# The check for experts over capacity placed in front of the last expert

## The chip, the cores and the metric

One core of one Trainium2 chip runs the whole program. The metric is device time in microseconds (us), the median over executions, and the reference's result has to be reproduced. An execution holds TensorE (PE, with its weight loads as PEld), VectorE (DVE), ScalarE (ACT), GpSimd (POOL) and SyncE (SP); SP issues nearly all the DMA transfers. A name with q behind it in a row (SPq, PEldq, DVEq, ACTq) is the instruction queue of that engine.

## The reference, cut to what matters

Two encoder layers over 256 tokens of width 1024. The first layer ends in a dense SwiGLU, the second in a layer of eight experts, of which each token uses two. The change lies in that expert layer:

```python
def moe_swiglu(h, router_w, w1, w3, w2):
    logits = (xf @ router_w).astype(jnp.float32)
    top_val, top_idx = lax.top_k(logits, TOP_K)          # 2 of 8 experts for each token
    gates = jax.nn.softmax(top_val, axis=-1)
    ...
    def expert_block(args):
        xblk, e = args
        return (jax.nn.silu(xblk @ w1[e]) * (xblk @ w3[e])) @ w2[e]
    ...
    out = jnp.zeros((n, d), h.dtype).at[buf_tok].add(yb * buf_g[:, None].astype(yb.dtype))
```

After it the layer's output is normalised, multiplied by a gate vector and added to the residual stream, which is the program's output.

## The kernel before, in words

The expert layer is `moe_layer`. Each of the eight experts has 42 pieces of weights of 1 MB. `weights` (L973) gives each piece a buffer and issues its DMA from SP (L978). The buffers form a ring of 18 in program order (L970): three and four that earlier stages used (`raw`, `hl`) and eleven of its own (`mw`).

An expert is planned for at most 96 tokens (`CAP`), in three groups of 32 slots. `gather` (L1040) makes its input: two DVE instructions build a one-hot matrix `oh`, 32 matmuls in four steps put the chosen tokens into `gx`, and eight ACT instructions write them, scaled and shifted, to `xe`. `oh` and `xe` have two buffers each.

The hidden width 3584 is worked through in four units `s` (L31: 256, 256, 256 and 128 columns of each of four parts of 896). `up` (L1104) multiplies `xe` with eight (in the last unit four) pieces of w1 and w3 into the accumulators `u`; `gated` (L1133) makes silu(a)*b on ACT and DVE and transposes it; `down` (L1145) multiplies that with four (at last two) pieces of w2 into `y`. `run` (L1230) is a pipeline: the `down` of a unit stands behind the `up` of the next unit, over the border between two experts as well. When the last `down` of an expert is out, `finish_tasks` splits `y` in two parts (`outputs`, L1167) and `back` (L1174) brings the slots back to token rows with 24 matmuls into `cb` and adds them, times the gate, to the sum `yac` on DVE (L1188). These tasks are given out between the pieces of the next expert's first `up`; those of the last expert come at the end.

The third group of slots is computed under a run-time branch on PE alone (`rest`, L1086, the branch at L1092): an expert with up to 64 tokens jumps over it.

`more` (L1258) hands further tasks to `run`: in the unit `s == 1` of each expert the gather of the next one (`prepare`), and in the first unit of the last expert the broadcast of the gate vector to `gtB`.

Experts with more tokens than 96 are handled by a general path. `count` makes a list of them; `over(0)` (L1276) loads its first entry into a register of every engine (L1277) and enters the branch `tc.If(ov > 0)` (L1278). Its body runs a whole expert again for the surplus, with its own gather and 42 pieces of weights, and holds `over(1)` up to `over(4)` inside, so the code of five experts stands in it. The body takes buffers of the same weight ring and of `oh`, `xe`, `u`, `y` and `yac`, in program order, whether it is entered or not. In the kernel before this call (L1303) stands behind all eight experts and in front of `residual` (L346): four ACT squares with row sums (`junk`, L299), 1/sqrt by Ln and Exp (L290, L291), four DVE products with `gtB` (L350), four DVE sums (L353) and the output DMAs (L355).

A planner orders the instructions of each engine by its own estimate of when they can start, so an instruction may stand earlier than in the program text when it needs nothing that comes in between; what is inside a branch is not mixed with what is outside.

Of the kernel before, what the change touches and what calls it, by code (L numbers as in the profile page):

```python
# [26 lines left out]
NE = 8  # L27
# [93 lines left out]
def kernel(ctx, tc, x, cc, cst, cst2, msk, ada, pcol, lora, poolw, rpb, win, winl, wout,  # L121
# [151 lines left out]
    def use_lnexp():  # L273

        pl = act.preload_act_table_set("natural_log_exp_and_others")
        if pin["last"] is not None:
            tc.add_manual_dep(pl.ins, pin["last"].ins.name, NOSYNC, reason="table set after its last user")
        pin["pl"] = pl
# [685 lines left out]
    def moe_layer(l):  # L964
        with ExitStack() as st:
# [74 lines left out]
            def gather(pos):  # L1040

                oh = ep.tile([128, 2, CAP], F32, name="oh", tag="oh", bufs=2)
                for tb in range(2):
                    dve.tensor_scalar(oh[:, tb, :], C("iota")[:, 0:CAP], pos[:, tb:tb + 1], rs[:, tb:tb + 1],
                                      op0=OP.is_equal, op1=OP.mult)
                xe = ep.tile([128, KB, CAP], F32, name="xe", tag="xe", bufs=2)

                def step(k2):
                    p = pa("gx").rearrange("p (j t) -> p j t", j=2)[:, :, 0:CAP]
                    for j in range(2):  # L1050
                        ks = slice((2 * k2 + j) * 128, (2 * k2 + j + 1) * 128)
                        for tb in range(2):
                            mm(p[:, j, :], xr[:, tb, ks], oh[:, tb, :], tb == 0, tb == 1)
                    for j in range(2):
                        k = 2 * k2 + j
                        act.activation(xe[:, k, :], p[:, j, :], AF.Identity,  # L1056
                                       scale=gcol[l][:, 2, k:k + 1], bias=mods[l][:, SH_F, k:k + 1])

                return xe, [lambda k2=k2: step(k2) for k2 in range(KB // 2)]
# [14 lines left out]
            def slot_map(x):  # L1074

                x.oT = one.tile([128, NG, T], F32R, name="oT", tag="oT")
                dve.tensor_tensor(x.oT, x.row[:, None, :].to_broadcast([128, NG, T]),
                                  C("slot")[:, :, None].to_broadcast([128, NG, T]), op=OP.is_equal)
# [25 lines left out]
            def up(x, s, tasks):  # L1104

                w = SUP[s]
                kk = 256 // w
                n0 = sum(KB * SUP[i] // 256 for i in range(s))
                us = [pb("u") for _ in range(NG)]

                def part(n, pc, gs):
                    for i in range(kk):
                        k = n * kk + i
                        for g in gs:
                            for j in range(4):
                                mm(us[g][32 * j:32 * j + 32, 0:2 * w],
                                   x.xe[:, k, 32 * g:32 * g + 32],
                                   pc((i * 4 + j) * 2 * w, 2 * w), k == 0, k == KB - 1)

                for m in range(0, KB // kk, BATCH):  # L1120
                    pcs_ = []
                    for n in range(m, m + BATCH):
                        pcs_.append((n, weights(x.src(n0 + n))))
                        part(*pcs_[-1], range(GB))
                        if tasks:
                            tasks.pop(0)()
                    x.rest(lambda: [part(n, pc, range(GB, NG)) for n, pc in pcs_],
                           (lambda: [clear(us[g]) for g in range(GB, NG)]) if m == 0 else None)
                while tasks:
                    tasks.pop(0)()  # L1130
                return us

            def gated(s, us):  # L1133
                w = SUP[s]
                sgs = []
                for u in us:
                    sg = ep.tile([128, 256], F32, name="sg", tag="sg", bufs=NG)[:, 0:w]
                    other_set(act.activation(sg, u[:, 0:w], AF.Silu))  # L1138
                    dve.tensor_mul(sg, sg, u[:, w:2 * w])  # L1139
                    sT = ep.tile([128, 256], F32, name="sT", tag="sT", bufs=2 * NG)[:, 0:w]  # L1140
                    dve.transpose(sT, sg)
                    sgs.append(sT)
                return sgs
# [46 lines left out]
            def finish_tasks(x, first):  # L1190
                outputs(x)
                return [lambda tb=tb: back(x, tb, first) for tb in range(2)]
# [27 lines left out]
            def fixed(e):  # L1220
                return lambda n: moe[e * NCH + n]
# [4 lines left out]
            def prepare(e):  # L1226
                xes[e], steps = gather(posm[:, :, e])
                return steps

            def run(units, extra_tasks=None):  # L1230

                prev = None
                tasks = []
                for x, s, first in units:
                    if s == 2:
                        slot_map(x)
                    if extra_tasks is not None:
                        tasks += extra_tasks(x, s)
                    us = up(x, s, tasks)
                    tasks = []  # L1240
                    aT = gated(s, us)
                    if prev is not None:
                        px, ps_, paT, pfirst = prev
                        down(px, ps_, paT)
                        if ps_ == len(SUP) - 1:
                            tasks = finish_tasks(px, pfirst)
                    prev = (x, s, aT, first)
                px, ps_, paT, pfirst = prev
                down(px, ps_, paT)
                for f in finish_tasks(px, pfirst):  # L1250
                    f()
# [5 lines left out]

            def more(x, s):  # L1258
                e = x.gi
                if s == 1 and e + 1 < NE:  # L1260
                    return prepare(e + 1)
                if e == 0 and s == 0:
                    return [lambda: rows_of(prow, posm, NE)]
                if e == NE - 1 and s == 0:
                    return [lambda: bcast_col(gtB, gcol[l][:, 3, :], pa)]
                return []

            def units():
                for e in range(NE):
                    x = Expert(fixed(e), prow[:, e, :], gate[:, :, e], e, xes[e], nt[0:1, e:e + 1])  # L1270
                    for s in range(len(SUP)):
                        yield x, s, e == 0

            run(units(), more)

            def over(i):  # L1276
                ov = nc.values_load(of[0:1, i:i + 1], min_val=0, max_val=1)  # L1277
                with tc.If(ov > 0):  # L1278
                    base = nc.sync.value_load(ox[0:1, i:i + 1], min_val=0, max_val=(NE - 1) * NCH)

                    def src(n):
                        return moe[bass.ds(base + n, 1)].rearrange("o p f -> p (o f)")

                    es = one.tile([128, NE], F32, name="es", tag="es")
                    dve.tensor_scalar(es, it8, oif[:, i:i + 1], None, op0=OP.is_equal)
                    pe2 = one.tile([128, 2, 2], F32, name="pe2", tag="pe2")
                    tmp = one.tile([128, NE], F32, name="etmp", tag="etmp")
                    for tb in range(2):
                        for q, a in ((0, posm), (1, gate)):
                            dve.scalar_tensor_tensor(tmp, a[:, tb, :], 1.0, es, op0=OP.mult, op1=OP.mult,  # L1290
                                                     accum_out=pe2[:, q, tb:tb + 1])
                    dve.tensor_scalar(pe2[:, 0, :], pe2[:, 0, :], osec[:, i:i + 1], None, op0=OP.subtract)
                    xe, steps = gather(pe2[:, 0, :])
                    for f in steps:
                        f()
                    orow = one.tile([128, 1, T], BF, name="orow", tag="orow")
                    rows_of(orow, pe2[:, 0, :, None], 1)
                    x = Expert(src, orow[:, 0, :], pe2[:, 1, :], NE + i, xe)
                    run(((x, s, False) for s in range(len(SUP))))
                    if i < NOV - 1:  # L1300
                        over(i + 1)

            over(0)  # L1303
            use_lnexp()
            residual([[yac[:, tb, h] for h in HALF] for tb in range(2)], out)

# [24 lines left out]
    if stop == 3:  # L1331
        nc.sync.dma_start(out, xr)
        return
    moe_layer(1)


# [118 lines left out]
```

## Time and profile before

| what | us |
|---|---|
| three runs | 1490.93, 1497.38, 1497.62 (median 1497.38) |
| profiled execution | 1491.34 |
| its span, first to last instruction | 1489.6 |
| PE, DVE, ACT busy | 1385.4, 610.0, 399.2 |
| expert layer's weights | 336 pieces of 1 MB |

The span is that of the profiled execution; its own time is 1.74 us longer. Busy PE time is modelled and includes matmuls that run half empty, so a high share of it does not say that PE is the bound of a stretch. Weights of the experts move from about 630 us on to 1470 us.

### The profile page before, as it was taken

What the parts mean: (1) busy time and instruction counts of PE and PEld (TensorE: products, weight loads), DVE (VectorE), ACT (ScalarE), POOL (GpSimd) and SP (SyncE); (2) the same over time, 40 slices, a digit from 0 to 9 for tenths busy, and PEclk for the clock granted to TensorE, in tenths of its full rate; (3) what the DMA queues carried; (4) which work ended last, traced back from release to release, by engine and by line L of the source; (5) the groups of instructions that cost most, each with busy time, mean ns of one, the idle gap of its engine ahead of it and who ended that gap; (6) DMA issues with size and microseconds to landing.
All of it is one profiled execution on the core that took longest, in us unless ns stands there. A gap on an engine that the chain in (4) does not pass through costs nothing. (4 is left out here: it accounts for less than half of the span.)

```text
span 1489.6 us, 30982 instructions
## 1 busy us (share of the span) xinstructions
PE 1385.4 (93%) x13669; PEld 818.1 (55%) x13694; DVE 610.0 (41%) x1198; ACT 399.2 (27%) x774; POOL 1.9 (0%) x19
## 2 busy tenths in 40 slices
PE   3999989999998999989998899999999999999874
PEld 2997769999997997743332233333333433333221
DVE  7698879878856786440020120021020200200203
ACT  4744465444437644231020010010010010010101
POOL 0000000000000000000000000000000000000000
PEclk9999999999999999999999999999999999999998
DMA  9554559977734420499999999999999999999993
GB/s 370 219 195 144 183 224 392 387 294 306 298 141 149 149 94 17 170 407 419 419 420 420 419 420 420 420 419 420 420 419 419 420 420 420 420 419 419 420 420 139
DMA packets 70286, 487.43 MB, mean 327 GB/s; under 512 B 8177, under 2 KB 8561, under 8 KB 12658
## 3 DMA queue, kind: packets, MB, share of 16 engines
q1 hardware_dynamic: 68546, 482.45, 80.1%
q10 hardware_dynamic: 1584, 2.68, 0.6%
q8 instruction: 125, 2.05, 0.5%
q14 instruction: 31, 0.25, 0.0%
HBM read 484.05 MB, written 1.05 MB: 326 GB/s over the span
## 5 line engine op out<-in xcount | busy, mean ns | idle before, releaser
L167 PE MATMUL u<-mw,xe 128*32 128x512 f32 (+1 forms) x4864 | 491.1, 541 | 24.0 <-DMA mw<-in_moe_dram 16.3
L167 PEld LDWEIGHTS u<-mw,xe 128*32 128x32 f32 x4864 | 157.8, 110 | 299.3 <-issue 237.8
L1139 DVE TENSOR_TENSOR sg<-sg,u 128x256 f32<-128x256 f32 (+1 forms) x96 | 34.0, 382 | 587.3 <-ACT sg L1138 587.3
L167 PE MATMUL y<-mw,sT 128*32 128x512 f32 x2128 | 243.0, 594 | 15.7 <-DMA mw<-in_moe_dram 10.3
L218 DVE TENSOR_TENSOR whl<-raw,whl 128x1024 fp32r<-128x1024 f32 x142 | 170.2, 1221 | 50.8 <-ACT whl L217 50.5
L1138 ACT ACTIVATE sg<-u 128x256 f32<-128x256 f32 (+1 forms) x96 | 30.7, 356 | 570.5 <-PE u L167 559.6
L217 ACT ACTIVATE whl<-raw 128x1024 fp32r<-128x1024 f32 x142 | 147.0, 1057 | 114.6 <-issue 51.5
L167 PEld LDWEIGHTS y<-mw,sT 128*32 128x32 f32 x2128 | 71.1, 110 | 174.4 <-issue 129.6
L170 PE MATMUL g<-hhi,whl 128*128 128x256 f32 x448 | 127.3, 284 | 0.0
L171 PE MATMUL g<-hlo,whl 128*128 128x256 f32 x448 | 127.2, 284 | 0.1
L172 PE MATMUL g<-hhi,whl 128*128 128x256 f32 x448 | 127.0, 284 | 0.0
L254 DVE CUSTOM_DVE_ANT_0 raw<-raw,row,pcs 128x1024 f32<-128x1024 f32 x96 | 120.2, 1278 | 4.6 <-ACT row L1311 3.9
L170 PE MATMUL z<-hhi,whl 128*128 128x256 f32 x304 | 88.1, 290 | 4.6 <-ACT whl L217 3.9
L172 PE MATMUL z<-hhi,whl 128*128 128x256 f32 x304 | 86.4, 284 | 2.4 <-DVE whl L218 2.4
L171 PE MATMUL z<-hlo,whl 128*128 128x256 f32 x304 | 86.6, 285 | 0.5 <-DVE hlo L336 0.3
L170 PEld LDWEIGHTS g<-hhi,whl 128*128 128x128 f32 x448 | 86.5, 193 | 0.6
L171 PEld LDWEIGHTS g<-hlo,whl 128*128 128x128 f32 x448 | 86.3, 193 | 0.8 <-DVE hlo L336 0.4
L172 PEld LDWEIGHTS g<-hhi,whl 128*128 128x128 f32 x448 | 86.3, 193 | 0.0
L170 PEld LDWEIGHTS z<-hhi,whl 128*128 128x128 f32 x304 | 58.0, 191 | 6.5 <-ACT whl L217 4.2
L172 PEld LDWEIGHTS z<-hhi,whl 128*128 128x128 f32 x304 | 58.0, 191 | 3.1 <-DVE whl L218 3.0
L171 PEld LDWEIGHTS z<-hlo,whl 128*128 128x128 f32 x304 | 58.1, 191 | 2.1 <-DVE hlo L336 1.1
L1056 ACT ACTIVATE xe<-gx,mods,gcol 128x96 f32<-128x96 f32 x64 | 24.1, 428 | 121.4 <-PE gx L167 121.2
(290 smaller groups left out, 1484.0 us busy)
## 6 DMA issues: line engine op xcount, KB each, us to landing
mw<-in_moe_dram SPq DMA_DIRECT2D x336, 1024.0 KB, 19.9
raw<-in_ada_dram SPq DMA_DIRECT2D x44, 1024.0 KB, 7.0
raw<-in_ffn_dram SPq DMA_DIRECT2D x42, 1024.0 KB, 7.2
raw<-in_win_dram SPq DMA_DIRECT2D x20, 1024.0 KB, 4.8
raw<-in_wout_dram SPq DMA_DIRECT2D x6, 1024.0 KB, 4.8
raw<-in_ada_dram SPq DMA_DIRECT2D x8, 512.0 KB, 7.4
bi<-in_rpb_dram ACTq DMA_DIRECT2D x8, 256.0 KB, 2.8
raw<-in_wout_dram SPq DMA_DIRECT2D x4, 512.0 KB, 3.6
```

Source lines behind the costliest of these rows:

```text
L167: pe.matmul(o, a, b, start=start, stop=stop)
L170: pe.matmul(o, ah, bh, start=start, stop=False)
L171: pe.matmul(o, ah, bl, start=False, stop=False)
L172: pe.matmul(o, al, bh, start=False, stop=stop)
L217: ops[0].append(act.activation(hi, raw[:, c], AF.Copy))
L218: ops[1].append(dve.tensor_sub(lo, raw[:, c], hi.bitcast(F32)))
L254: r = dve.tensor_tensor_reduce(w, w, cB, scale=1.0, scalar=P(l, "ab", v * KB + k), op0=OP.mult, op1=OP.add, accum_out=mods[l][:, v, k:k + 1])
L1056: act.activation(xe[:, k, :], p[:, j, :], AF.Identity, scale=gcol[l][:, 2, k:k + 1], bias=mods[l][:, SH_F, k:k + 1])
L1138: other_set(act.activation(sg, u[:, 0:w], AF.Silu))
L1139: dve.tensor_mul(sg, sg, u[:, w:2 * w])
```

## The change

`over(0)` is called after seven experts instead of after eight. The pipeline `run` is called twice: once for the experts 0 to 6 and once for the expert 7. Between the two stand the check and the gather of expert 7, whose four steps are called one after another; before, they were handed out among the pieces of expert 6. Nothing is computed differently.

```diff
             def more(x, s):
                 e = x.gi
-                if s == 1 and e + 1 < NE:
+                if s == 1 and e + 1 < NE - 1:
                     return prepare(e + 1)
...
-            def units():
-                for e in range(NE):
+            def units(es):
+                for e in es:
                     x = Expert(fixed(e), prow[:, e, :], gate[:, :, e], e, xes[e], nt[0:1, e:e + 1])
                     for s in range(len(SUP)):
                         yield x, s, e == 0
-
-            run(units(), more)
...
+            run(units(range(NE - 1)), more)
             over(0)
+            for f in prepare(NE - 1):
+                f()
+            run(units(range(NE - 1, NE)), more)
             use_lnexp()
             residual([[yac[:, tb, h] for h in HALF] for tb in range(2)], out)
```

## Rows read from the trace of the kernel before

**Rows 1.** The page: span, the DMA line of the 40 slices, the weight transfers

```profile
span 1489.6 us, 30982 instructions
...
DMA  9554559977734420499999999999999999999993
...
mw<-in_moe_dram SPq DMA_DIRECT2D x336, 1024.0 KB, 19.9
```

**Rows 2.** Busy time by stretch; last: PE clock, DMA share, GB/s

```profile
800.00:900.00 100.00, 90.39 (x850) 30.15 (x847) 13.61 (x32) 7.81 (x21) 0.00 (x0) 1.00 1.01 420
1300.00:1400.00 100.00, 93.86 (x852) 34.74 (x854) 15.81 (x35) 9.86 (x25) 0.00 (x0) 1.00 1.01 419
```

**Rows 3.** Waits of SP's queue: total us, times, longest

```profile
SPq L978 <- DMA mw<-in_moe_dram: 582.9, 285, 3.7
...
SPq L978 <- PEq L1092: 9.6, 4, 6.9
```

**Rows 4.** Timeline, end of the last expert: start, us, what, idle before

```profile
1458.11 1.92 PE L167 MATMUL y<-mw,sT 128*32 128x512 f32 x16 [0.55 <-DMA mw<-in_moe_dram]
...
1470.59 1.93 PE L167 MATMUL y<-mw,sT 128*32 128x512 f32 x16 [0.46 <-SPq L1278]
...
1473.10 2.99 PE L167 MATMUL cb<-yhl,oT 64*128 64x512 f32 x22 [0.16 <-DVE yhl L1172]
...
1474.80 2.73 DVE L1188 SCALAR_TENSOR_TENSOR yac<-cb,gate,yac 128x512 f32<-128x512 f32 x4 [0.90 <-PE cb L167]
1479.83 0.63 ACT L299 ACTIVATE junk<-yac 128x512 bf16<-128x512 f32 x1 [4.82 <-DVEq L1278]
```

**Rows 5.** The check's line L1278 by engine: duration ns, first and last start

```profile
L1278 SPq EVENT_SEMAPHORE  x9: 17/17/17, 1455.8 to 1470.8; - x9
...
L1278 PEldq EVENT_SEMAPHORE  x2: 51/51/51, 1477.9 to 1478.0; - x2
L1278 DVEq EVENT_SEMAPHORE  x2: 21/21/21, 1479.8 to 1479.9; - x2
...
L1278 SPq COMPARE_BRANCH  x1: 45/45/45, 1450.5 to 1450.5; - x1
...
L1278 PEldq COMPARE_BRANCH  x1: 3370/3370/3370, 1474.4 to 1474.4; - x1
L1278 DVEq COMPARE_BRANCH  x1: 72/72/72, 1476.8 to 1476.8; - x1
```

**Rows 6.** The weight DMAs of L978, issue to landing over all 336

```profile
DMA to landing us min/median/max: 4.8/19.9/21.5
```

**Rows 7.** Timeline, tail after the check on DVE and SP

```profile
1480.59 0.69 DVE L350 TENSOR_TENSOR yac<-yac,row 128x512 f32<-128x512 f32 x1 [3.06 <-ACT junk L299]
...
1482.68 0.68 DVE L350 TENSOR_TENSOR yac<-yac,row 128x512 f32<-128x512 f32 x1
...
1483.29 2.73 DVE L353 SCALAR_TENSOR_TENSOR xr<-yac,rs,xr 128x512 f32<-128x512 f32 x4
```

**Rows 8.** Timeline, the first expert's gather: DVE, then PE

```profile
643.41 0.56 DVE L1044 TENSOR_SCALAR oh<-cs,posm,rs 128x96 f32<-128x96 f32 x2
643.78 5.44 PE L167 MATMUL gx<-oh,xr 128*128 128x96 f32 x32 [0.71 <-DVE oh L1044]
```

**Rows 9.** Timeline of expert 6 on PE, and its border to expert 7

```profile
1302.89 1.13 PE L167 MATMUL gx<-oh,xr 128*128 128x96 f32 x8
...
1323.98 1.16 PE L167 MATMUL bc<-cs,gcol 128*128 128x128 f32 x8
...
1331.91 7.08 PE L167 MATMUL u<-mw,xe 128*32 128x512 f32 x64 [0.25 <-issue]
...
1369.58 1.92 PE L167 MATMUL u<-mw,xe 128*32 128x512 f32 x16 [0.55 <-DMA mw<-in_moe_dram]
```

**Rows 10.** Busy time by stretch at the end; third last: PE clock

```profile
1478.00:1480.00 2.00, 0.00 (x0) 0.00 (x0) 0.00 (x0) 0.17 (x1) 0.00 (x0) 1.00 0.03 8
1480.00:1482.00 2.00, 0.00 (x0) 0.00 (x0) 1.42 (x4) 2.00 (x8) 0.00 (x0) 0.66 0.01 4
1482.00:1484.00 2.00, 0.00 (x0) 0.00 (x0) 1.95 (x5) 1.17 (x5) 0.00 (x0) 0.50 0.00 0
```

## The prediction

> **What bounds the kernel now.** I read the page first. Its DMA line stands at 9 in the slices from about 17 to 39: from some 630 us on the core does nothing faster than it can load weights, 336 pieces of 1 MB [rows 1]. The table by stretches says the same in numbers: the DMA share is 1.01 at 419 to 420 GB/s in any 100 us of the expert layer [rows 2], so a piece of 1.049 MB costs 2.50 us. The timeline of the last expert shows it from the other side. PE needs 1.92 us for a piece and then waits for the next one; from the pieces that start at 1458.11 to the one at 1470.59 there are five steps, 12.48 / 5 = 2.50 us each [rows 4]. SP issues a piece when one of eight in flight has landed (285 waits for the transfers themselves), and only rarely waits for a buffer [rows 3]; eight times 2.50 us are the 19.9 us that a piece takes to land [rows 1]. So the layer's time is that of an unbroken stream of transfers, and whatever PE, ACT and DVE do in it is free until it breaks the stream. Last I read the rows of the check's own line and the tail, where the stream has ended and everything is exposed [rows 4, 5, 7].
>
> **What the check does where it stands now.** No instruction of the body was executed: no expert is over capacity, each engine jumps. The jump isn't free. PE meets it at 1474.4 while its last matmuls still run, is held 3.37 us, and signals at 1477.9 that it is past. DVE meets it at 1476.8 and signals at 1479.8. SP is the first, at 1450.5, and then executes nine event instructions, the last at 1470.8, just when the last piece has landed: it waits there for its transfers in flight, one after another [rows 5]. And later work waits for these signals as if the body had run. ACT's first square needs the sum `yac`, whose first quarter is finished by 1475.5, but starts at 1479.83, released by DVE's signal [rows 4].
>
> **Part 1, the check out of the tail: a gain of 3.0 us.** Without it the squares start as the quarters of `yac` arrive. ACT could so begin 1479.83 - 1475.5 = 4.3 us earlier, but DVE can't follow: its four sums L1188 last until 1474.80 + 2.73 = 1477.53 [rows 4], and behind them stand the products and sums of the residual, which run from 1480.59 without a real gap to 1483.29 + 2.73 = 1486.02 [rows 7]. That 5.4 us block now starts when DVE is free and at least one square has read its quarter, so at about 1477.55 instead of 1480.59: 3.0 us. What is late next is DVE itself. Bounds: 0, if the residual's order changes for the worse, and 4.3. The load of the ACT table that stands there now lies beside DVE's sums and stays so.
>
> **Part 2, the check between experts 6 and 7: a loss of 9.6 us.** Every weight DMA of expert 7, 42 of them, is now behind the check in SP's queue, and behind it in the buffers too: the ring's last users in program order are the matmuls of the body. The rows give two possible ends of SP's wait. Its own events, 0.2 us after the last piece (1470.8 against 1470.59) [rows 4, 5], are the lower one. The upper one is the signal of an engine that uses the buffers, that is PE: 1477.9 - 1470.59 = 7.3 us after the last piece of the expert begins on PE. I take PE's. It is what happened to ACT with DVE's signal [rows 4], and SP's weight DMAs are already seen waiting for PE's signal at the small branch L1092, four times, up to 6.9 us [rows 3]. If SP had to wait for the slowest engine, DVE, it would be 9.2 us.
>
> Then the queue is empty. A piece that meets an empty queue lands 4.8 us after its issue, the smallest of the 336 values [rows 6]. So expert 7's first piece is there 7.3 + 4.8 = 12.1 us after the last piece of expert 6, where the unbroken stream needed 2.50. The difference is 9.6 us. All 41 others follow at 2.50 us, so this is shifted to the end in full. Nothing of the 10 us is won back by the buffers that are free: they can't be filled before PE's signal. Bounds by SP's wait: 0.2 + 4.8 - 2.5 = 2.5 us and 9.2 + 4.8 - 2.5 = 11.5 us.
>
> The chain between last piece and signal is the one seen at the end, with expert 6 in place of expert 7: matmuls, `outputs`, 24 matmuls of `back` ending at 1476.09, the jump. Before, these lay between the pieces of expert 7. Expert 6 could enter it late: PE works there without waiting for weights and meets the stream again at 1369.58 in expert 7 [rows 9]. But PE loses work in expert 6, the gather of 32 matmuls (four times 1.13 us [rows 9]), so I expect it level with the stream; the bound is some 1.5 us more.
>
> [...] PE was held 3.37 us by the jump [rows 5], and its matmuls in the queue ended 1.8 us before the signal. [...]
>
> **Part 3, the gather of expert 7: nothing.** In expert 6 its matmuls filled time under the stream, so taking them out there gives nothing. In the new place it waits for DVE's signal at +9.2 us, then 0.56 us for `oh` and 5.4 us for 32 matmuls [rows 5, 8]: PE is ready at about +15.2 us, 3.1 us after the first piece. It catches up: unhindered it takes 7.08 / 4 = 1.8 us for a piece [rows 9] against 2.50, so 0.7 us a piece, five pieces of 42. [...] The broadcast to `gtB` was moved by the planner into expert 6 already [rows 9] and is free in either place.
>
> **Sum.** -3.0 + 9.6 + 0 = +6.6 us. On the profiled execution's own time, 1491.34 (span 1489.6 and 1.74 around it), that is 1497.9, or 0.44% more. The three runs lie in two groups, one like the profiled execution, two some 6.2 us above it; nothing in the profile says which the changed kernel will meet, so I put the sum on their mean, 1495.3: 1501.9.
>
> **Rivals.**
> - SP waits only for its own transfers. For it: the nine events are the only thing SP is seen waiting for at L1278. Against: ACT's wait for DVE's signal. Then 2.5 - 3.0 = -0.5, 1494.8.
> - The planner takes expert 7's weights past the check, so that the stream isn't broken: it does move work past small branches, as the `bc` row inside expert 6 shows [rows 9]. Against: buffers of the ring that the body uses. Then -3.0, 1492.3. It is the only faster case, and less than 0.5%.
> - The tail doesn't give back its 3.0 us, since DVE puts the residual in another order or waits for the last square. Then +9.6, 1504.9.
> - Slower still, by PE: the gather behind the jump becomes the bound. It is exposed after DVE's signal, and it decides if PE can't win back its delay before the last piece, that is if a piece of expert 7 costs PE 2.4 us or more, as with the third group of slots computed. Then 3.1 (or, at the lower clock, 8.5) comes on top: +9.7 to +15.1, 1505.0 to 1510.4. Against: at the end of expert 7 PE needs 1.92 us a piece [rows 4]. [...]
>
> **How the numbers follow.** Chances: forecast 0.60, SP free of PE 0.10, stream unbroken 0.05, tail without gain 0.13, PE's delay 0.12. A measurement of this kernel tells about 0.5% (7.5 us) from no change. The forecast lies 0.9 us below that line, with its own range from +5 (a cheaper jump) to +8.5 (SP held to DVE's signal), so about 0.4 of its chance is slower and the rest the same. Slower: 0.60 x 0.4 + 0.13 + 0.12 = 0.49, of which I take off a little for the two groups of runs, which can hide it: 0.45. Faster by over 0.5% is reached by no case, 0.05 for what I don't see. Same 0.50. The range leaves out the unbroken stream below and the slowest form of PE's delay by a little: 1494 to 1511.
>
> **What would show it.** In the changed profile: SP's events of the check's line near 1365 us and then no weight issue until PE's second signal, some 7 us later; a hole in the DMA line of about 10 us; in the tail, squares that start on `yac` itself and DVE going from L1188 to L350 without its 3.06 us pause. The prediction is wrong if weights are issued before PE's signal, if PE waits less than 0.3 us for pieces at the end of expert 7, or if the hole is under 6 or over 13 us.

## The result and the profile after

| | before | changed |
|---|---|---|
| median of 12 runs each, us | 1496.38 (1490.93 to 1497.62) | 1504.01 (1499.34 to 1506.82) |
| ratio | | 1.0056, 95% interval 1.0045 to 1.0068 |
| profiled execution, us | 1491.34 | 1505.6 |
| its span, us | 1489.6 | 1503.8 |

The change makes the kernel 7.6 us slower by the medians, 8.4 by the ratio (6.7 to 10.2 by the interval); +6.6 us and 1501.9 had been forecast. The two profiled executions lie 14.2 us apart, which is more than the change does. So the stages are compared from one instruction that both kernels have before they differ, the first of expert 5's `cb` matmuls. It stands at 1291.79 before and at 1296.70 after: the first 4.9 us of the 14.2 have nothing to do with the change.

```profile
1291.79 1.60 PE L167 MATMUL cb<-yhl,oT 64*128 64x512 f32 x6
```

```profile
1296.70 1.60 PE L167 MATMUL cb<-yhl,oT 64*128 64x512 f32 x6
```

From there to PE's start on the last piece of weights it takes 178.80 us before (1470.59 [rows 4]) and 191.24 after (1487.94, below): +12.4. From there to the end of the span 19.0 and 15.9: -3.1. Together +9.3 in this pair of executions.

The page of the changed kernel, the lines that answer to [rows 1]:

```profile
span 1503.8 us, 31010 instructions
...
DMA  9554459987734420499999999999999999995995
...
mw<-in_moe_dram SPq DMA_DIRECT2D x336, 1024.0 KB, 19.9
```

The row of nines has a 5 in it. The busy time by stretch shows what it is (columns as in [rows 2], the last ones PE clock, DMA share and GB/s):

```profile
1300.00:1365.00 65.00, 60.99 (x586) 20.28 (x582) 9.58 (x23) 2.80 (x9) 0.00 (x0) 1.00 0.95 391
1365.00:1378.00 13.00, 7.73 (x64) 3.56 (x56) 4.80 (x7) 1.79 (x3) 0.00 (x0) 1.00 0.13 50
```

For 13 us the core loads 50 GB/s in place of 420. The check's line, now L1276, answers to [rows 5]:

```profile
L1276 SPq EVENT_SEMAPHORE  x9: 17/17/17, 1355.0 to 1370.2; - x9
...
L1276 PEldq EVENT_SEMAPHORE  x2: 51/51/51, 1377.1 to 1377.2; - x2
L1276 DVEq EVENT_SEMAPHORE  x2: 21/21/21, 1379.1 to 1379.3; - x2
...
L1276 SPq COMPARE_BRANCH  x1: 50/50/50, 1349.9 to 1349.9; - x1
...
L1276 PEldq COMPARE_BRANCH  x1: 3333/3333/3333, 1373.7 to 1373.7; - x1
```

And the timeline of the border between the experts 6 and 7 (start, us, engine, line, idle before with its releaser):

```profile
1363.53 1.93 PE L167 MATMUL y<-mw,sT 128*32 128x512 f32 x16 [0.56 <-DMA mw<-in_moe_dram]
...
1369.81 1.92 PE L167 MATMUL y<-mw,sT 128*32 128x512 f32 x16 [0.47 <-SPq L1276]
...
1377.17 42.49 SPq L978 DMA_DIRECT2D mw<-in_moe_dram  x23
1379.45 0.57 DVE L1044 TENSOR_SCALAR oh<-cs,posm,rs 128x96 f32<-128x96 f32 x2 [2.71 <-DVEq L1276]
1379.92 6.75 PE L167 MATMUL gx<-oh,xr 128*128 128x96 f32 x32 [4.61 <-DVE oh L1044]
...
1386.51 1.98 PE L167 MATMUL bc<-cs,gcol 128*128 128x128 f32 x16
...
1388.42 5.36 PE L167 MATMUL u<-mw,xe 128*32 128x512 f32 x48
...
1402.00 1.92 PE L167 MATMUL u<-mw,xe 128*32 128x512 f32 x16 [0.56 <-DMA mw<-in_moe_dram]
```

PE begins the last piece of expert 6 at 1369.81. SP's own transfers have all landed by 1370.2, but it issues nothing until 1377.17, right behind PE's first signal at 1377.1. What released it is named in SP's waits of that stretch (us in total, times, longest):

```profile
SPq L1276 <- SPq L1276: 19.9, 3, 12.3
SPq L978 <- PEq L1276: 6.8, 1, 6.8
```

When expert 7's first piece landed can be seen by SP's ninth issue, which waits for it, alone in its window of the timeline:

```profile
1384.55 0.33 SPq L978 DMA_DIRECT2D mw<-in_moe_dram  x1
```

That is 7.4 us after the issue at 1377.17, where 4.8 had been counted. PE takes the piece up at 1388.42, 3.9 us later, behind the gather, and waits for the stream again from 1402.00 on.

The tail (answers to [rows 4, 7]):

```profile
1487.94 1.92 PE L167 MATMUL y<-mw,sT 128*32 128x512 f32 x16 [0.46 <-DMA mw<-in_moe_dram]
...
1492.15 1.41 DVE L1188 SCALAR_TENSOR_TENSOR yac<-cb,gate,yac 128x512 f32<-128x512 f32 x2 [0.90 <-PE cb L167]
1492.93 0.63 ACT L299 ACTIVATE junk<-yac 128x512 bf16<-128x512 f32 x1 [2.41 <-DVE yac L1188]
...
1493.69 0.69 DVE L350 TENSOR_TENSOR yac<-yac,row 128x512 f32<-128x512 f32 x1
...
1495.03 1.40 DVE L1188 SCALAR_TENSOR_TENSOR yac<-cb,gate,yac 128x512 f32<-128x512 f32 x2
...
1498.94 1.41 DVE L353 SCALAR_TENSOR_TENSOR xr<-yac,rs,xr 128x512 f32<-128x512 f32 x2
```

The squares are released by the sums themselves, and DVE doesn't stand still for 3 us any more.

### The profile page after: what moved, and what is told of

Its sections match the earlier page's. It is cut to its first block, busy times and chain, and to the rows that moved or that the text cites. A ratio compares the mean times of both kernels' runs of the same rounds, so it can differ in the third digit from the quotient of the medians.

```text
span 1503.8 us, 31010 instructions
## 1 busy us (share of the span) xinstructions
PE 1400.7 (93%) x13694; PEld 830.7 (55%) x13694; DVE 610.0 (41%) x1198; ACT 399.3 (27%) x774; POOL 1.9 (0%) x19
```

## The experiments

Two theories about the loss. The first: SP's queue is held at the check until PE signals, the stream of weights runs dry, and the restart comes on top. The rival: the cut pipeline and the late gather cost it, on PE. A third, a fixed price of emptying the queue whatever PE does, differs from the first in where the price comes from. "Stretch" is the time from the `cb` row of expert 5 to the start on the last piece, "tail" from there to the end of the span, both of the profiled execution.

| kernel | stretch, us | tail, us | ratio to before, interval |
|---|---|---|---|
| before | 178.80 | 19.0 | 1 |
| changed | 191.24 | 15.9 | 1.0056 (1.0045 to 1.0068) |
| no check | 178.82 | 16.0 | 0.9977 (0.9965 to 0.9990) |
| check at the end, pipeline cut | 178.68 | 18.8 | 0.9994 (0.9982 to 1.0007) |
| body on its own buffers | 183.91 | 15.9 | 0.9999 (0.9983 to 1.0016) |
| small body | 187.92 | 16.3 | 1.0045 (1.0028 to 1.0062) |
| gather early | 190.43 | 15.7 | 1.0050 (1.0027 to 1.0073) |
| check in front of expert 4 | - | 15.8 | 1.0186 (1.0142 to 1.0229) |
| body on its own buffers and GpSimd's queue | 178.69 | 15.5 | 0.9973 (0.9957 to 0.9990) |

**No check.** In the kernel before:

```diff
-            over(0)
             use_lnexp()
```

> The kernel before, with the check and its general path left out (experts over capacity would lose tokens). Theory (the check in the tail costs what DVE stands still between its last sum into yac and the residual, and nothing in the stream): 3.1 us less than before, ratio 0.998, the tail from the last piece of weights to the end of the span 15.9 us as in the changed kernel, against 19.0. Rival (the tail's gain of the changed kernel comes from another order of the residual, not from the check): no change, tail 19.0 us.

The stretch is that of before, the tail 3.0 us shorter, the ratio 0.9977. It is the check that costs the tail its 3 us; where it stood before, it costs the stream nothing.

**The pipeline cut, the check at the end.** In the changed kernel:

```diff
             run(units(range(NE - 1)), more)
-            over(0)
             for f in prepare(NE - 1):
                 f()
             run(units(range(NE - 1, NE)), more)
+            over(0)
```

> The changed kernel with the check put back behind expert 7; the pipeline stays cut in two and the gather of expert 7 stays behind expert 6. Theory (all of the loss is the check's hold on SP): same as before within 1.5 us, and no hole in the weight stream between experts 6 and 7. Rival (the cut pipeline and the exposed gather cost it): 9 to 12 us slower than before, as the changed kernel with its tail gain taken off.

The stretch is 178.68, the ratio 0.9994. The rival falls: cutting the pipeline and putting the gather behind `back` costs nothing while the stream goes on. The gather there, at the full clock:

```profile
1370.11 3.81 PE L167 MATMUL gx<-oh,xr 128*128 128x96 f32 x32
```

**The body on buffers of its own.** In the changed kernel, with `only` as a key of `mw`, and the ring set to its start for expert 7, so that its first seven pieces go to `raw` and `hl`:

```diff
-                kind = ring[mw["n"] % len(ring)]
+                kind = mw["only"] or ring[mw["n"] % len(ring)]
...
+            mw["only"] = "mw"
             over(0)
+            mw.update(only=None, n=0)
```

> The changed kernel, but the check's body uses the eleven own buffers alone, and expert 7 begins with the seven others, which the body does not touch. Theory (SP's first weights wait for PE's signal only because the body's matmuls are the last readers of those buffers): first weights of expert 7 issued 0.3 to 0.5 us after the last piece of expert 6 has landed instead of 7.4, so the stream's hole shrinks by 7 us; 7 us faster than the changed kernel, 0 to 2 us slower than before. Rival (the hole is PE's own: late gather, late start): same as the changed kernel, 7.6 us slower than before.

The loss in the stretch falls from 12.4 to 5.1 us: the 7 us are gone as the first theory has it. Less the tail's 3.1 that leaves 2.0 us in the profiled executions; the ratio is 0.9999, and its interval reaches to 2.4 us. The way is another than expected. The planner, free of the body's buffers, put four issues of expert 7 in front of the check, the first at 1362.80:

```profile
1362.80 26.05 SPq L978 DMA_DIRECT2D mw<-in_moe_dram  x14
```

Its line of the check:

```profile
L1276 SPq EVENT_SEMAPHORE  x9: 17/17/17, 1370.1 to 1379.7; - x9
...
L1276 PEldq EVENT_SEMAPHORE  x2: 51/51/51, 1379.4 to 1379.6; - x2
...
L1276 SPq COMPARE_BRANCH  x1: 50/50/50, 1364.8 to 1364.8; - x1
```

SP's nine events end at 1379.7, when these four pieces have landed, and only then the next one is issued, at 1379.80, to an empty queue. PE signalled at 1379.4, a little before, and the next buffer is one that the body doesn't touch, so here it is the own transfers that hold SP.

**The body on its own buffers and on GpSimd's queue.** The same, and for the body alone:

```diff
-                nc.sync.dma_start(t, src)
+                (pool if mw["only"] else nc.sync).dma_start(t, src)
...
-                    base = nc.sync.value_load(
+                    base = pool.value_load(
```

> The kernel with the check's body on the eleven own buffers, and the body's weights issued from GpSimd's queue instead of SP's; the check in front of expert 7, which begins with the seven other buffers. Theory (what is left of the hole is SP waiting at the check until its own transfers have landed, since the body would use the same transfer semaphores): SP goes past the check without a wait for transfers, the first seven pieces of expert 7 follow at 2.5 us and the rest are released by PE's signal before these have landed; no hole, only the tail's 3.1 us are left: 0.998 of before, 1492 us. Rival (SP is held anyway, or the fetch of instruction pages beside the stream costs several us): 1 to 5 us slower than that, same as before.

SP has one event at the check instead of nine and goes on at once; its wait for PE's signal is still there, but the pieces issued before cover it. Check line, SP's waits, and the stretch in which the changed kernel loaded 50 GB/s:

```profile
L1276 PEldq EVENT_SEMAPHORE  x2: 51/51/51, 1380.2 to 1380.4; - x2
...
L1276 SPq COMPARE_BRANCH  x1: 50/50/50, 1365.4 to 1365.4; - x1
L1276 SPq EVENT_SEMAPHORE  x1: 17/17/17, 1365.6 to 1365.6; - x1
```

```profile
SPq L978 <- PEq L1276: 7.4, 1, 7.4
```

```profile
1365.00:1378.00 13.00, 7.94 (x64) 3.56 (x56) 4.80 (x7) 1.79 (x3) 0.00 (x0) 1.00 1.00 415
```

The stretch is that of before (178.69), the tail the short one, the ratio 0.9973. With the check in the place of the change, this kernel is faster than both, by 3.6 us against before in the two profiled executions (178.80 + 19.0 against 178.69 + 15.5); it can't be told from the kernel without a check. No run here enters the body, so what GpSimd's queue would cost it then is not shown.

**A small body.** In the changed kernel the body of the check becomes

```python
                    for n in range(len(ring)):
                        pc = weights(src(n))
                        mm(pa("sb"), pc(0, 128), pc(0, 512))
```

> The changed kernel with another body of the check: eighteen pieces loaded into the ring and one matmul on each, in place of up to five experts (experts over capacity would lose tokens); nothing to jump far over. Theory (PE's hold at the jump and the late first piece are both instruction pages that must be fetched, the latter on one of the sixteen DMA engines): PE signals 5.6 us after the last piece instead of 7.4, the first piece lands 4.8 us after issue instead of 7.3; 4.3 us faster than the changed kernel. Rival (the first piece is late because seven others are issued right behind it): PE's 1.8 us alone. Rival (the jump's length does not matter): same as the changed kernel.

The check's line and SP's ninth issue:

```profile
L1276 PEldq COMPARE_BRANCH  x1: 330/330/330, 1372.5 to 1372.5; - x1
L1276 PEldq EVENT_SEMAPHORE  x1: 51/51/51, 1374.2 to 1374.2; - x1
```

```profile
1374.23 11.08 SPq L978 DMA_DIRECT2D mw<-in_moe_dram  x11
```

```profile
1379.04 0.33 SPq L978 DMA_DIRECT2D mw<-in_moe_dram  x1
```

PE begins the last piece of expert 6 at 1368.61 here, so its signal comes 5.6 us after that (changed: 7.3), with a jump of 0.33 us in place of 3.33; and the first piece has landed 4.8 us after its issue. Both are as expected. But the stretch gains only 3.3 us on the changed kernel, not 4.3: the trace's landing events put the second piece at 1382.48, 3.5 us after the first instead of 2.5. The delay that the first piece escaped hit the second by 1 us. So the jump's length costs PE 1.7 us (7.3 against 5.6, one execution each; the ratios, 1.0045 and 1.0056, overlap too widely to show it). That the restart's extra is instruction pages in the transfers' way is not shown: in front of expert 4 (below), over the large body, the restart was as cheap as here.

**The gather early.** In the changed kernel expert 7's gather goes back to the unit `s == 1` of expert 6, with `oh` and `xe` tiles of its own:

```diff
-                if s == 1 and e + 1 < NE - 1:
+                if s == 1 and e + 1 < NE:
...
             over(0)
-            for f in prepare(NE - 1):
-                f()
```

> The changed kernel with the gather of expert 7 back among the pieces of expert 6, in buffers of its own; the check stays in front of expert 7. Theory (the gather behind the check is hidden, since PE works off its delay against the stream within expert 7): same as the changed kernel within 1 us, 1.0056 of before, although PE starts on expert 7's first piece as soon as it lands. Rival (the late gather is part of the price): 4 us faster than the changed kernel, the time by which PE comes late to the first piece.

The stretch is 0.8 us shorter than that of the changed kernel, the ratio 1.0050 against 1.0056 with intervals that overlap widely. PE takes the first piece as it lands, at 1376.85 by the landing events, and then waits for the next two:

```profile
1376.98 2.12 PE L167 MATMUL u<-mw,xe 128*32 128x512 f32 x16
1380.21 1.92 PE L167 MATMUL u<-mw,xe 128*32 128x512 f32 x16 [1.12 <-DMA mw<-in_moe_dram]
1383.19 1.92 PE L167 MATMUL u<-mw,xe 128*32 128x512 f32 x16 [1.06 <-DMA mw<-in_moe_dram]
```

It gains nothing by it. Of the 0.8 us 0.7 lie in the landings themselves, that is in the restart of the queue and not in the gather (numbers under Part 2 below).

**The check in front of expert 4.** In the changed kernel the same two lines with 4 for the border, and no gather for expert 4 in expert 3 (that condition in `more` is left out here):

```diff
-            run(units(range(NE - 1)), more)
+            run(units(range(4)), more)
             over(0)
-            for f in prepare(NE - 1):
+            for f in prepare(4):
                 f()
-            run(units(range(NE - 1, NE)), more)
+            run(units(range(4, NE)), more)
```

> The changed kernel with the check in front of expert 4 instead of expert 7 (experts 2 and 3 have over 64 tokens, so PE runs some 20 us behind the weight stream at the end of expert 3, and level with it at the end of expert 6). Theory (SP is held until PE signals that it is past the check): the hole in the stream grows by PE's delay, from 12 to about 32 us, 27 to 30 us slower than before. Rival (SP is held by its own transfers and the restart of an empty queue, a fixed price): the same hole as in the changed kernel, 7 to 9 us slower than before.

Medians 1521.14 (two runs) and 1495.87, 25 us apart; by the ratio, 1.0186, it is 28 us slower. SP's waits of the stretch, and the check's line:

```profile
SPq L978 <- PEq L1276: 27.1, 1, 27.1
```

```profile
L1276 SPq EVENT_SEMAPHORE  x9: 17/17/17, 1038.5 to 1052.6; - x9
...
L1276 PEldq EVENT_SEMAPHORE  x2: 51/51/51, 1079.7 to 1079.9; - x2
```

SP's own transfers have landed at 1052.6; the wait for PE lasts until 1079.8 because PE still has pieces of expert 3 to work off that have lain in their buffers. A fixed price falls: the hole is as long as PE is late.

## Why the prediction was right

**Part 1, the check out of the tail.** Forecast -3.0, measured -3.1 in the profile and -3.0 by leaving the check out. The reason holds, that DVE and not ACT sets the gain: the pause that went is DVE's 3.06 us [rows 7]. In detail it came otherwise: the block of products and sums doesn't start behind the four sums L1188. The planner put the first half of the residual between the first two and the last two of them (L350 at 1493.69, L1188 again at 1495.03).

**Part 2, the hold on SP.** The choice between the two ends of SP's wait was the step that decided, and it was right: 7.3 us from the last piece to PE's signal were forecast from the end of expert 7 and 7.3 were measured at the end of expert 6 (1369.81 to 1377.1, PE's first signal; the list of signs in the prediction says the second). Of the two reasons given, ACT's wait for DVE's signal and SP's for PE's at L1092, the second is the very same mechanism; with buffers of its own for the body it no longer stood before the first pieces, and in front of expert 4 it stretched to 27.1 us.

The term that was mis-sized is the restart: "A piece that meets an empty queue lands 4.8 us after its issue, the smallest of the 336 values". It took 7.3 us here by the landing events, and the loss of 12.4 us is above the prediction's own upper bound of 11.5. Fifteen of the piece's sixteen parts were there by 1381.99, 4.8 us after the issue, and the last at 1384.49. What held that part the trace doesn't say; the profile's list of DMA queues has three transfers of instructions between 1377 and 1385. Three engines jump within 4 us at this place (ACT at 1372.3, PE at 1373.7, DVE at 1376.0), but that this delays the part is not shown.

The step that follows was wrong too: "All 41 others follow at 2.50 us". Five of the kernels have a hole. The table gives how long after its issue the first piece landed, and the price when the stream is steady again: the tenth landing after that issue, less nine steps of 2.49 us.

| kernel | first piece, us | price at the tenth, us |
|---|---|---|
| changed | 7.3 | 7.3 |
| gather early | 5.3 | 6.6 |
| small body | 4.8 | 6.1 |
| check in front of expert 4 | 5.3 | 6.1 |
| body on its own buffers | 5.1 | 7.0 |

So the first piece can land after 4.8 us, but then some of the next four come late, and no restart came under 6.0 us. The sum was 1.3 to 2.5 us short by this term. Each value is from one execution, and the cause of the spread stays open. In the changed kernel's profile the stream lost 12.4 us instead of 9.6, and the sum of this pair of executions is +9.3 instead of +6.6. The twelve runs' 7.6 lie between.

**Part 3, the gather.** Nothing was forecast, and of the 0.8 us that the gather in its old place gives, 0.7 are the restart's. The gather began after TensorE had stood idle for 4.6 us, ran mostly at the lower clock (0.50 from 1380 to 1386, the level that the tail before ends at [rows 10]; third last column) and took 6.75 us:

```profile
1382.00:1384.00 2.00, 2.00 (x11) 2.00 (x11) 0.00 (x0) 1.10 (x4) 0.00 (x0) 0.50 0.99 397
```

The value counted, 5.4 us, was not that of the full clock: the row of 5.44 [rows 8] was itself taken at a mean clock of 0.76 (643 to 650 us), and at the full clock, with the check at the end, the same 32 matmuls took 3.81. PE was 3.9 us late and level again with the eighth piece. The 8.5 us that the slowest rival adds "at the lower clock", and with them the upper end of the range, are shown by no run; the 6.75 and the 3.9 us of the changed kernel are what was measured. One reading was not as said: the broadcast to `gtB` did not stay inside expert 6, it stood behind the check too, 1.98 us of PE at 1386.51. The same slack hid it.

**PE's hold at the jump.** PE's jumps over the check's body took 3.33 to 3.83 us over the large body in these traces with the queue empty, as in [rows 5], and 0.33 us over the small one. The lower end of the forecast's own range, "+5 (a cheaper jump)", no run shows for the large body; over the small one PE's signal came 5.6 us after the last piece, against 7.3. At the small branch L1092 of the kernel before, PE's 121 records have a median of 0.18 us (min/median/max in ns):

```profile
L1092 PEldq COMPARE_BRANCH  x121: 65/179/2372, 655.9 to 1468.3; - x121
```

What fills the 3.33 to 3.83 us no row shows.

**Readings that were off.** SP does not "only rarely" wait for a buffer: in the kernel before, 53 of its waits in front of a weight DMA end with PE's matmuls on `u` or `y`, 96 us together, against 582.9 us for transfers [rows 3]. The DMA share of 1.01 [rows 2] shows that they don't break the stream, so the sum stands.

```profile
SPq L978 <- PE u L167: 67.8, 39, 10.6
...
SPq L978 <- PE y L167: 28.5, 14, 5.7
```

And SP is not the first at the check: GpSimd met it at 651.1 us. Nothing hangs on it.

**The rivals.** SP free of PE and the unbroken stream did not come by themselves, since the body's buffers stood against both, as argued; each was brought about by taking that reason away. The tail gave back its gain, and PE's delay decided nothing.

**The line of 0.5%.** Of the 2.1 us between 1501.9 and 1504.0, 1.1 are the base, which had been taken from three runs, and 1.0 the change. By the medians 7.6 us is 0.1 us above the line, and the forecast was 0.9 below; the slower case had been given 0.45 and the middle one 0.50. On which side it fell is close to chance; the term of the restart, 1.3 to 2.5 us too small, is large enough to have tipped it.

## What to carry to other kernels

In this program a run-time branch that isn't taken is still a joint for SP's queue: what stands behind it there waits until PE, which would have used the shared buffers, has come past it (6.8 us here, 27.1 in front of expert 4), so on a stream-bound kernel it belongs where the stream is over, or its body must share neither the buffers nor the queue of what follows (with both apart SP had one event at the check, at 1365.6; in the changed kernel it had nine, the last at 1370.2). When a wait is moved, look for the engine whose signal ends it and ask how late that engine is at the new place; other buffers and another queue for a body that never ran were worth 12 us here (0.9973 against 1.0056), and the place alone was worth 20 us of SP's wait (27.1 against 6.8). Price the restart after a hole by the landings of several pieces, not by the fastest single one in the trace.

## What was not expected of the hardware

The hold at the jump goes with the traffic: 3.33 to 3.83 us in the five kernels whose weight queue had run dry when PE jumped over the large body, 5.97 and 6.03 us in the two kernels in which pieces were in flight:

```profile
L1276 PEldq COMPARE_BRANCH  x1: 5973/5973/5973, 1373.4 to 1373.4; - x1
```

```profile
L1276 PEldq COMPARE_BRANCH  x1: 6033/6033/6033, 1374.1 to 1374.1; - x1
```

The first is that of the body on its own buffers, the second the one with GpSimd's queue besides. In the second the longer hold costs nothing, since seven pieces cover it. That the traffic causes it is not shown.

SP's record of the branch is 50 ns, but its first event comes 5.1 us later in the changed kernel (1349.9 to 1355.0), and 0.2 us later where the body issues nothing from SP (1365.4 to 1365.6). What fills that time is not shown; in the changed kernel the transfers in flight cover it.

Two executions of what is the same program up to there differed by 5 us before the weights of the experts had begun to stream, whose first DMA is issued at 597.1 us before and at 602.3 after: that is where the 4.9 us between the two `cb` rows come from. The mean granted clock of the span doesn't explain it: it is 0.991 in the profiled execution before and 0.986 after, but 0.991 as well in that of the kernel without a check, whose first weights are issued at 601.7.
